# A hybrid attention and recurrence block: rotary key in two passes, cleared corners instead of a cleared tile, table loads and conditioning row rearranged

## The chip, the cores and the metric

The kernel runs on one core of a Trainium2 chip. The metric is the device time of one execution in microseconds; lower is better. The profiled execution gives a trace of every engine: TensorE (PE, with its weight loads PEld), VectorE (DVE), ScalarE (ACT), GpSimd (POOL) and SyncE (SP), which here issues nearly all DMAs.

## The reference

One layer of a block on 512 latent tokens and 256 context tokens, width 1024, all in fp32. The parts that matter here:

```python
h  = modulate(rmsnorm(x, g_norm_mix), sh1, sc1)      # mod = silu(c) @ w_mod + b_mod
cq, ckv, kpe, hq, hi, hg, ff, fb = split(h @ w_in)   # and the same for the context
# group A: latent attention, 4 heads; kpe (64 wide) is one rotary key for all heads
k_lat = full_k(kn_l, apply_rope(kpe_l, cos, sin), N) # the context's kpe is not rotated
k_ctx = full_k(kn_c, kpe_c, L)
# group B: gated linear recurrence, 4 heads, 2 directions, chunks of 64 tokens
A = einsum('bthk,bshk->bhts', qc * exp(b - b_ref), kc * exp(b_ref - b))
A = where(mask, A, 0.0)
o = rmsnorm(o_fwd + o_bwd, g_on) * silu(hg)
x = x + gt1 * (concat([o_mla, o_hgrn]) @ w_out)
x = x + gt2 * swiglu(modulate(rmsnorm(x, g_norm_ffn), sh2, sc2), w_gate, w_up, w_down)
out = rmsnorm(x, g_final)
```

`apply_rope` takes pairs of features 16 apart within 32 and rotates them by the angle of the token's row or column in the grid.

## The kernel before

**Precision by splitting.** Activations and weights stand with features on the 128 partitions. A matmul operand is split into a rounded part (hi, written by ScalarE as a cast to fp32r) and the rest (lo, written by VectorE as a difference). `mm3` (L148 to L152) multiplies hi x hi, hi x lo and lo x hi: three matmuls for one product. `make_unit` (L119) loads a weight unit of 128 x 1024 by a DMA on SyncE's queue (L122), casts it on ScalarE (L132) and takes the difference on VectorE (L133); the three tiles stand in rings of three buffers. `unit(i)` asks for two units ahead.

**Order.** The program is written in one order, and a scheduler then places each instruction in its engine's queue, by the priority of its place in the program and by when it expects it to be ready; `prio` moves a few up or down. On the chip each queue runs in order. So a line that stands far below can come early if it depends on little. PSUM gives two pairs of banks (`big`) and four single banks (`sm`).

**Stages.** (1) 0 to 65 us: modulation of the mix, the norm, h split into `hh`, `hl` (latent) and `gh`, `gl` (context). (2) 65 to 300 us: projections. `hgrn_q`, `gates` and `mla_kpe` call `project` (L452 to L465), which runs 8 k-steps; each step has three matmuls of 512 columns and three of 256. Between the steps `tick` advances generators: `hgrn_dir` (one head, one direction), `hgrn_out` (one head), `mla_feats`. (3) 300 to 360 us: scores, softmax and values of the attention, four heads. (4) the output projection, the second norm, the feed-forward layer, the last norm.

**The masked scores in `hgrn_dir`.** `pa` is a PSUM bank of four blocks of 128 x 128, each with two chunks of 64 x 64 on its diagonal. L549 multiplies a zero matrix (`zr`) by 512 columns of `hh` and so writes zero into all of the bank. Then 16 small fp32 matmuls (L555), each with 32 columns of the array and 64 or 32 columns of output, add the scores of each chunk; of each chunk one corner of 32 x 32 isn't computed, since the mask empties it. L559 copies the masked part to `am[d]`; the rest of `am` stays zero. `hgrn_out` adds the two directions on GpSimd (L592), multiplies by the values (L598 and L604), and norms (`rstd_cols`, L610 to L614); L620 turns the result round.

**`rstd_cols`** computes 1/sqrt on a few columns. With `fast` ScalarE takes a square root (L190), and VectorE takes the reciprocal and one Newton step: five VectorE instructions. Without it VectorE does all: three on the integer bits, then three Newton steps of three: twelve. Here `fast` is on in the last head only.

**The rotary key, `mla_kpe` (L709 to L720).** The last unit of `w_in` (KPU) has 128 columns: the 64 of kpe, and the same 64 with features exchanged 16 apart. One `project` gives both. VectorE multiplies the first half by cos (L713) and the second by sin (L714), ScalarE moves the second to the partitions of the first (L715), VectorE adds them (L716). Then the result is split into `krh` (L719) and `krl` (L720), for latent and context apart and into both halves of the partitions.

**The conditioning row.** `scx` holds silu(c) on all partitions, 128 x 1024, in the place of the cos and sin tables. L433 loads c as a broadcast, L434 and L435 make silu of it; `late_mod` (L422 to L429) then multiplies rows of `w_mod` by it, one row of 128 x 1024 each. After 12 of these the tables are loaded over it (L746). When the queries are rotated (L786 to L794) c is loaded again and silu made again (L812 to L815), for the other 20.

**Function tables of ScalarE.** Sigmoid, Exp, Sqrt and Silu need different tables; a table load precedes the first use after another. Two lines are there to load a table early: L818 (Exp, before the softmax) and L1037 (Sqrt, before the last norm).

## Time and profile before

| | |
|---|---|
| median of 3 runs (lowest to highest) | 793.59 us (791.45 to 795.61) |
| profiled execution: its time | 792.62 us |
| its span (first to last instruction) | 790.8 us |
| mean granted clock of TensorE | 0.988 |
| instructions: TensorE, VectorE, ScalarE | 4342, 820, 569 |
| DMA traffic | 88.77 MB |

The page of a profile gives busy times by engine, a picture of the span in 40 slices, the chain of work that ended last (followed back from the end, at each step to what released it), and groups of instructions by line. Further views give the same for a stretch of time: busy time of each engine, who waited for whom, and single instructions in order. A matmul's recorded length overlaps with its neighbours; the distance from one start to the next is what a matmul costs in a full stream.

### The profile page before, as it was taken

What the parts mean: (1) busy time and instruction counts of PE and PEld (TensorE: products, weight loads), DVE (VectorE), ACT (ScalarE), POOL (GpSimd) and SP (SyncE); (2) the same over time, 40 slices, a digit from 0 to 9 for tenths busy, and PEclk for the clock granted to TensorE, in tenths of its full rate; (3) what the DMA queues carried; (4) which work ended last, traced back from release to release, by engine and by line L of the source; (5) the groups of instructions that cost most, each with busy time, mean ns of one, the idle gap of its engine ahead of it and who ended that gap; (6) DMA issues with size and microseconds to landing.
All of it is one profiled execution on the core that took longest, in us unless ns stands there. A gap on an engine that the chain in (4) does not pass through costs nothing.

```text
span 790.8 us, 10832 instructions
## 1 busy us (share of the span) xinstructions
PE 768.1 (97%) x4342; PEld 631.7 (80%) x4342; DVE 446.9 (57%) x820; ACT 311.4 (39%) x569; POOL 10.1 (1%) x18
## 2 busy tenths in 40 slices
PE   8899999999999989999999999999999999999995
PEld 7568878788887768888999888888888888888885
DVE  5576569839778989985566434432333233223324
ACT  6344246434544577664344223222322222212211
POOL 0000000000000100000000000000000000000000
PEclk8899999999999999999999999999999999999997
DMA  9923723311110022345403343423232323332303
GB/s 332 390 76 134 252 80 108 133 57 55 64 55 28 28 80 90 125 165 181 160 2 100 113 160 133 151 89 107 80 107 82 104 78 96 93 100 80 111 3 107
DMA packets 26706, 88.77 MB, mean 112 GB/s; under 512 B 2976, under 2 KB 5280, under 8 KB 26528
## 3 DMA queue, kind: packets, MB, share of 16 engines
q1 hardware_dynamic: 25568, 87.03, 33.0%
q10 hardware_dynamic: 1088, 1.05, 0.4%
q8 instruction: 34, 0.56, 0.3%
q14 instruction: 16, 0.13, 0.1%
HBM read 85.97 MB, written 2.10 MB: 111 GB/s over the span
## 4 chain that ended last, share of the span: by engine, by line
PE 89%; DVE 7%; ACT 2%; issue 1%; DMA 1%; SPq 0%; DVEq 0%; ACTq 0%
PE big L150 18%; PE big L151 17%; PE big L152 17%; PE sm L150 9%; PE sm L151 9%; PE sm L152 9%; PE big L857 2%; PE sm L604 1%; PE sm L876 1%; PE big L858 1%; PE sm L320 1%; DVE U L585 1%; PE sm L598 1%; DVE acl L309 1%; DVE G L506 1%
## 5 line engine op out<-in xcount | busy, mean ns | idle before, releaser
L133 DVE TENSOR_TENSOR wl<-wf,wh 128x1024 fp32r<-128x1024 f32 (+2 forms) x100 | 119.6, 1196 | 186.3 <-ACT wh L132 186.2
L132 ACT CAST wh<-wf 128x1024 fp32r<-128x1024 f32 (+2 forms) x100 | 102.9, 1029 | 280.3 <-PE big L151 167.6
L150 PE MATMUL big<-h2h,wh 128*128 128x512 f32 (+1 forms) x368 | 140.3, 381 | 0.0
L151 PE MATMUL big<-h2l,wh 128*128 128x512 f32 (+1 forms) x368 | 140.0, 381 | 0.0
L152 PE MATMUL big<-h2h,wl 128*128 128x512 f32 (+1 forms) x368 | 140.0, 381 | 0.0
L151 PEld LDWEIGHTS big<-h2l,wh 128*128 128x128 f32 x368 | 69.2, 188 | 14.6
L150 PEld LDWEIGHTS big<-h2h,wh 128*128 128x128 f32 x368 | 69.2, 188 | 14.4
L152 PEld LDWEIGHTS big<-h2h,wl 128*128 128x128 f32 x368 | 69.2, 188 | 14.4
L150 PE MATMUL sm<-ah,wh 128*128 128x512 f32 (+1 forms) x198 | 73.5, 371 | 0.0
L152 PE MATMUL sm<-ah,wl 128*128 128x512 f32 (+1 forms) x198 | 73.4, 371 | 0.0
L151 PE MATMUL sm<-al,wh 128*128 128x512 f32 (+1 forms) x198 | 73.4, 370 | 0.0
L427 DVE SCALAR_TENSOR_TENSOR wl<-wl,cs 128x1024 f32<-128x1024 f32 x32 | 39.0, 1220 | 33.8 <-DMA wl<-in_wmt_dram 33.8
L150 PE MATMUL big<-wh,hh 128*128 128x512 f32 x96 | 40.2, 422 | 3.3 <-ACT hh L340 1.9
L150 PEld LDWEIGHTS sm<-ah,wh 128*128 128x128 f32 x198 | 37.3, 188 | 7.1
L151 PEld LDWEIGHTS sm<-al,wh 128*128 128x128 f32 x198 | 37.3, 188 | 7.1
L152 PEld LDWEIGHTS sm<-ah,wl 128*128 128x128 f32 x198 | 37.3, 188 | 7.1
L150 PE MATMUL big<-hh,wh 128*128 128x512 f32 x104 | 42.8, 412 | 0.0
L151 PE MATMUL big<-hl,wh 128*128 128x512 f32 x104 | 40.9, 394 | 0.0
L152 PE MATMUL big<-hh,wl 128*128 128x512 f32 x104 | 40.8, 392 | 0.0
L151 PE MATMUL big<-wl,hh 128*128 128x512 f32 x96 | 38.8, 406 | 0.0
L152 PE MATMUL big<-wh,hl 128*128 128x512 f32 x96 | 38.4, 402 | 0.0
L506 DVE RECIPROCAL G<-S 128x528 f32<-128x528 f32 x8 | 27.5, 3432 | 0.1
(326 smaller groups left out, 1353.4 us busy)
## 6 DMA issues: line engine op xcount, KB each, us to landing
wf<-in_wgu_dram SPq DMA_DIRECT2D x44, 512.0 KB, 3.4
wl<-in_wmt_dram SPq DMA_DIRECT2D x32, 512.0 KB, 3.5
wf<-in_wi_dram SPq DMA_DIRECT2D x25, 512.0 KB, 3.9
wf<-in_wd_dram SPq DMA_DIRECT2D x16, 512.0 KB, 3.5
wms<-in_wm_dram SPq DMA_DIRECT2D x11, 512.0 KB, 9.6
wf<-in_wo_dram SPq DMA_DIRECT2D x8, 512.0 KB, 3.5
wf<-in_wd_dram SPq DMA_DIRECT2D x8, 384.0 KB, 3.1
wm<-in_wm_dram SPq DMA_DIRECT2D x5, 512.0 KB, 10.2
```

The costliest lines, as they stand in the source:

```text
L132: nc.scalar.copy(hi[:, :w], f[:, :w])
L133: nc.vector.tensor_sub(lo[:, :w], f[:, :w], hi[:, :w].bitcast(F32))
L150: nc.tensor.matmul(o, lh, rh, start=start, stop=False, skip_group_check=True)
L151: nc.tensor.matmul(o, lh, rl, start=False, stop=False, skip_group_check=True)
L152: nc.tensor.matmul(o, ll, rh, start=False, stop=stop, skip_group_check=True)
L309: nc.vector.tensor_add(acc_, acc_, sq_)
L320: nc.tensor.matmul(ps[32 * g : 32 * g + 32, :256], csil[:, 4 * j + kk, :], f[:, kk * 256 : (kk + 1) * 256], start=(j == 0), stop=(j == 1), ...
L427: nc.vector.scalar_tensor_tensor(f, f, 1.0, sc, op0=ALU.mult, op1=ALU.mult, accum_out=acc)
L506: nc.vector.reciprocal(I, S)
L585: nc.vector.scalar_tensor_tensor(U[:, c1, :], U[:, c0, :], er[:, 1, c0 : c0 + 1], U[:, c1, :], op0=ALU.mult, op1=ALU.add)
L598: nc.tensor.matmul(t, a2[:, j, :], vt[:, j, h * P : (h + 1) * P], start=True, stop=False, skip_group_check=True)
L857: nc.tensor.matmul(ps[:, 0, :], L, R[:, :NL], start=(i == 0), stop=(i == 4), skip_group_check=True)
```

## The change

- **Rotary key.** The KPU unit holds only the 64 columns of kpe, and its hi and lo parts stand side by side in one tile of 128 columns per k-step. Two matmuls instead of three (by `hh` and by `hl`, or `gh` and `gl`) give the hi products on the lower 64 partitions and the lo products on the upper 64; the sum of both halves is the key, now with lo x lo as well. The exchange of features 16 apart is a shuffle on VectorE behind it, and latent and context are split together, 768 columns at a time. An Exp with scale 0 into a spare column follows the rotation.
- **Corners.** Instead of L549 two bf16 matmuls with zeros write the corner blocks alone, and the small matmuls overwrite instead of adding. The masked copy is made for the two diagonal quarters apart.
- **Norm of the last head.** `fast` is off.
- **Conditioning row.** After the first silu one row of it goes to a scratch row in DRAM; the second load reads that row as a broadcast, and the second Sigmoid and product go, with the Exp behind them (L818).
- **L1037** goes.

```diff
@@ units, make_unit
-        units.append(("wi", wi[u], UNIT))
+        units.append(("wi", wi[u], UNIT) if u < NW_IN - 1 else ("kp", wi[u][:, : UNIT // 2], UNIT // 2))
...
-        nc.scalar.copy(hi[:, :w], f[:, :w])
-        nc.vector.tensor_sub(lo[:, :w], f[:, :w], hi[:, :w].bitcast(F32))
+        if kind == "kp":
+            f3 = f[:, :w].rearrange("p (k c) -> p k c", c=64)
+            h3 = hi.rearrange("p (k s c) -> p k s c", s=2, c=64)
+            nc.scalar.copy(h3[:, :, 0], f3)
+            nc.vector.tensor_sub(h3[:, :, 1], f3, h3[:, :, 0].bitcast(F32))
+        else:
+            nc.scalar.copy(hi[:, :w], f[:, :w])
+            nc.vector.tensor_sub(lo[:, :w], f[:, :w], hi[:, :w].bitcast(F32))
@@ conditioning row, first time
+    srow = tc.dram_tile([1, DM], F32, name="srow")
...
     nc.vector.tensor_mul(scx, scx, scs)
+    nc.sync.dma_start(srow, scx[0:1, :])
...
-    zr = HG.tile([P, P], F32R, name="zr")
-    nc.gpsimd.memset(zr.bitcast(F32), 0.0)
+    zr = HG.tile([P, P], F32, name="zr")
+    nc.gpsimd.memset(zr, 0.0)
     zc = zr.bitcast(BF16)
@@ hgrn_dir
         pa = sm()
-        nc.tensor.matmul(pa, zr, hh[:, 0, :], start=True, stop=False, skip_group_check=True)
+        for g in (1 - d, 3 - d):
+            c0 = (g // 2) * CH + 32 * d
+            nc.tensor.matmul(pa[32 * g : 32 * g + 32].rearrange("p (j t) -> p j t", t=P)[:, :, c0 : c0 + 32],
+                             zc[:, 0:32], zc[:, 0:P].rearrange("p (j t) -> p j t", t=32), start=True, stop=True,
+                             skip_group_check=True, tile_position=(0, 32 * g))
...
-                                 start=False, stop=True, skip_group_check=True, tile_position=(0, 32 * g))
+                                 start=True, stop=True, skip_group_check=True, tile_position=(0, 32 * g))
         with prio(100):
             p4 = pa.rearrange("p (j t) -> p j t", t=P)
-            nc.vector.copy_predicated(am[d], mk[:, d : d + 1, :].to_broadcast([P, 4, P]), p4)
+            for g in range(2):
+                r = slice(g * CH, (g + 1) * CH)
+                nc.vector.copy_predicated(am[d][r, :, r], mk[r, d : d + 1, r].to_broadcast([CH, 4, CH]), p4[r, :, r])
@@ hgrn_out
-        rr, _ = rstd_cols(HG, (ss, 4), P, fast=h == NH - 1)
+        rr, _ = rstd_cols(HG, (ss, 4), P)
@@ mla_kpe
-        ps = project(KPU)
-        kp = HG.tile([P, NL], F32, tag="q", name=nm("kp"), bufs=2)
-        m = HG.tile([P, NL], F32, tag="sg", name=nm("kpm"), bufs=2)
-        nc.vector.tensor_mul(kp[0:64, :], ps[0:64, :NL], C("cos")[0:64, :])
-        nc.vector.tensor_mul(kp[64:128, :], ps[64:128, :NL], C("sin")[64:128, :])
-        nc.scalar.copy(m[0:64, :], kp[64:128, :])
-        nc.vector.tensor_add(kp[0:64, :], kp[0:64, :], m[0:64, :])
-        for src, c in ((ps[0:64, NL:NT], slice(NL, NT)), (kp[0:64, :], slice(0, NL))):
-            for r in (slice(0, 64), slice(64, 128)):
-                nc.scalar.copy(krh[r, c], src)
-                nc.vector.tensor_sub(krl[r, c], src, krh[0:64, c].bitcast(F32))
+        w, _ = unit(KPU)
+        ps = big()
+        for k in range(KT):
+            for i in range(2):
+                for o, n, t in ((ps[:, 0, :], NL, (hh, hl)), (ps[:, 1, :NC], NC, (gh, gl))):
+                    nc.tensor.matmul(o, w[:, k * P : (k + 1) * P], t[i][:, k, :n], start=(k == 0 and i == 0),
+                                     stop=(k == KT - 1 and i == 1), skip_group_check=True)
+            if k in (1, 4):
+                tick()
+        ps = ps.rearrange("p a b -> p (a b)")
+        kp = HG.tile([P, NT], F32, tag="kk", name=nm("kp"), bufs=3)
+        m = HG.tile([P, NT], F32, tag="sg", name=nm("kpm"), bufs=2)
+        nc.scalar.copy(m[0:64, :], ps[64:128, :NT])
+        nc.vector.tensor_add(kp[0:64, :], ps[0:64, :NT], m[0:64, :])
+        nc.vector.stream_shuffle(m[0:64, :NL], kp[0:64, :NL], SWAP)
+        nc.vector.tensor_mul(kp[0:64, :NL], kp[0:64, :NL], C("cos")[0:64, :])
+        nc.vector.tensor_mul(m[0:64, :NL], m[0:64, :NL], C("sin")[0:64, :])
+        nc.vector.tensor_add(kp[0:64, :NL], kp[0:64, :NL], m[0:64, :NL])
+        nc.scalar.activation(epst2[0:64, :], m[0:64, 0:1], AF.Exp, scale=0.0)
+        for r in (slice(0, 64), slice(64, 128)):
+            nc.scalar.copy(krh[r, :], kp[0:64, :])
+            nc.vector.tensor_sub(krl[r, :], kp[0:64, :], krh[0:64, :].bitcast(F32))
@@ behind make_qr
-    nc.sync.dma_start(scx, cin.rearrange("(o c) -> o c", o=1).to_broadcast([P, DM]))
-    scs = HG.tile([P, DM], F32, tag="U", name="scs", bufs=2)
-    nc.scalar.activation(scs, scx, AF.Sigmoid)
-    nc.vector.tensor_mul(scx, scx, scs)
+    nc.sync.dma_start(scx, srow.to_broadcast([P, DM]))
     lim_[0] = 32
     wq_n = unit(QU + 2, 1)
-    nc.scalar.activation(epst2, scs[:, 0:1], AF.Exp)
@@ before the last norm
-    nc.scalar.activation(epst2, epst, AF.Sqrt)
@@ host: the last unit of w_in
-    wi += [_tiles(np.concatenate([kp, kp[:, swap]], axis=1))[0]]
+    wi += [np.zeros((P, UNIT), np.float32)]
+    wi[-1][:, : UNIT // 2] = kt(part["kpe"]).reshape(P, UNIT // 2)
```

3 lines of the change are left out of this document (removed).

## The prediction

> **What bounds the kernel now.** I read the page first: busy time, then the chain of work that ended last.
>
> ```profile
> PE 768.1 (97%) x4342; PEld 631.7 (80%) x4342; DVE 446.9 (57%) x820; ACT 311.4 (39%) x569; POOL 10.1 (1%) x18
> ...
> PE 89%; DVE 7%; ACT 2%; issue 1%; DMA 1%; SPq 0%; DVEq 0%; ACTq 0%
> ```
>
> TensorE is busy 97% of the span and makes up 89% of the chain, so matmul time taken out should come off the end, except where another engine sets the pace. The places that the change touches lie between 100 and 303 us, so I read busy time by stretch there (columns after the stretch and its length: busy us of TensorE, its weight loads, VectorE, ScalarE, GpSimd, each with its count of instructions; then the granted clock, the DMA share, and GB/s).
>
> ```profile
> 100.00:231.00 131.00, 129.71 (x897) 107.52 (x897) 100.74 (x196) 59.21 (x132) 2.57 (x2) 1.00 0.25 79
> ...
> 251.40:271.00 19.60, 17.96 (x177) 14.58 (x173) 18.99 (x43) 10.20 (x31) 1.27 (x1) 1.00 0.02 5
> 271.00:285.00 14.00, 13.98 (x77) 10.02 (x79) 12.93 (x26) 7.83 (x16) 2.30 (x3) 1.00 0.21 68
> 285.00:293.50 8.50, 6.36 (x29) 4.17 (x26) 7.56 (x17) 7.91 (x18) 0.00 (x0) 1.00 0.42 136
> ```
>
> Up to 231 us TensorE is full (129.71 of 131 us) and VectorE has room (100.74). From 251.4 to 285 VectorE is as full as TensorE (31.92 and 31.94 of 33.6 us). From 285 to 293.5 all three engines leave gaps: waits in a row, not one full engine. The granted clock is 1.00 throughout. Who TensorE waits for from 225 to 310 us (waiter, releaser: total us, times, longest):
>
> ```profile
> PE big L150 <- DVE krl L720: 1.6, 1, 1.6
> PE sm L620 <- DVE ow L614: 1.2, 1, 1.2
> PE big L857 <- ACT pp L863: 1.1, 1, 1.1
> PE big L150 <- DVE qnl L776: 1.0, 2, 0.7
> ```
>
> All four name VectorE or ScalarE. The chain of waits agrees: between these two pieces (start, us, what) it stays on VectorE, for 19.5 us, and goes on on TensorE.
>
> ```profile
> 251.44 0.70 DVE qg L531
> ...
> 270.49 0.43 DVE krl L720
> ```
>
> **The change part by part.**
>
> *Clearing the corners of the masked scores (L549).* This runs eight times. Today a 512-column multiplication by zeros comes before the 16 small ones; the chain shows it as follows (start, us, what).
>
> ```profile
> 130.15 0.24 PE sm L549
> 130.39 0.58 PE sm L555 x22
> 130.97 0.43 PE big L150
> ```
>
> L549 puts 0.24 us on the chain. It goes; two bf16 clears of 128 columns come, each on a quarter of the array's columns. No row shows such an instruction. From above: the two cost as much as L549 and the gain is nothing; a loss I exclude, since together they send half of its columns. From below: L555's 16 multiplications take 0.58 us, two of that kind 0.07; and L150 behind L555 takes 0.43 where L549, as wide, takes 0.24, so a change of kind costs some 0.19, which may go too. I take 0.11 for the two, nearest to L555, whose tile positions they share: 0.13 us saved each time. Five of the eight lie where TensorE sets the end (130 to 228 us): 5 x 0.13 = **0.65 us**, bounds 0 to 5 x (0.24 - 0.07 + 0.19) = 1.8. The copy behind it (L559, 0.71 us in the table of VectorE below) becomes two of 64 x 256; by the 256-wide L720 (0.412) that is 0.82, or 0.11 more VectorE time each.
>
> *Rotary key in two passes.* One of eight k-steps of the projection today, its first matmul and that of the next step:
>
> ```profile
> 255.99 0.39 PE L150 MATMUL big<-hh,wh 128*128 128x512 f32 x1
> ...
> 257.03 0.40 PE L150 MATMUL big<-hh,wh 128*128 128x512 f32 x1
> ```
>
> Six matmuls take 1.04 us; four take two thirds, 0.69. Over eight steps 0.35 x 8 = 2.8 us of TensorE go. But they lie at 251 to 264 us, where VectorE is the chain. So VectorE's bill decides. Its rows (mean ns of one is the last number before the next bar):
>
> ```profile
> L559 DVE COPY_PREDICATED am<-mk,sm 128x512 f32<-128x512 int32 x8 | 5.7, 710 | 0.0
> ...
> L861 DVE TENSOR_REDUCE ast<-big 128x1 f32<-128x768 f32 x4 | 3.8, 950 | 0.9 <-PE big L858 0.9
> ...
> L182 DVE SCALAR_TENSOR_TENSOR rsr<-rst,rsr 128x4 f32<-128x4 f32 x16 | 2.6, 161 | 0.3
> ...
> L716 DVE TENSOR_TENSOR kp<-kp,kpm 64x512 f32<-64x512 f32 x1 | 1.4, 1416 | 0.0
> ...
> L720 DVE TENSOR_TENSOR krl<-kp,krh 64x512 fp32r<-64x512 f32 x2 | 1.4, 685 | 0.0
> ...
> L788 DVE SCALAR_TENSOR_TENSOR m<-m,cs 128x512 f32<-128x512 f32 x2 | 1.4, 682 | 0.0
> ...
> L815 DVE TENSOR_TENSOR cs<-cs,scs 128x1024 f32<-128x1024 f32 x1 | 1.2, 1212 | 0.0
> ...
> L720 DVE TENSOR_TENSOR krl<-big,krh 64x256 fp32r<-64x256 f32 x2 | 0.8, 412 | 0.0
> ```
>
> Out: L713 and L714 (512 wide, as L788: 0.68 each), L716 1.416, L720 twice 0.412 and twice 0.685: 5.0 us. In: the sum of the halves over 768 columns (as L861, 0.95), a shuffle, two products and a sum of 512 (as L788, 0.68 each), two differences of 768 (0.95 each): 5.6 us. That is +0.6. ScalarE's copies grow from 2048 to 2304 columns in all, and a table load joins them; ScalarE is busy 10.20 of 19.60 us there, which hides both. What queues behind that load are the copies of the key and of the values (L802); if the cover were gone, it would cost the load's 1.28 us and some 0.3 for the columns. The KPU unit's split is half as wide: it falls near 222 us, where both engines have room, so I count nothing. A gain no instruction shows: today the PSUM pair of the projection is held until the last L720 that reads it, and TensorE waits 1.6 us for that; after, the first sum frees it.
>
> L716's 1.416 us is twice a 512-wide sum (L788 0.682), and this stands beside it:
>
> ```profile
> 267.18 1.27 POOL L592 TENSOR_TENSOR a<-am,am 128x512 f32<-128x512 f32 x1 [27.58 <-DVE am L559]
> ```
>
> The sum of head 3 ran on GpSimd from 267.18 to 268.45, and L716 from 267.58: they met. [...]
>
> *Last head's norm without the square root.* `rstd_cols` in head 3 goes from one ScalarE and five VectorE steps to twelve VectorE steps of 0.16 us (L182): seven more, 1.12 us if nothing lies between, about half of that when they alternate with long instructions. I count +0.5. The step is on the path: L614 at 293.02 needs it, and TensorE waits 1.2 us at L620 for L614.
>
> *Conditioning row and table loads.* ScalarE's rows:
>
> ```profile
> 287.49 1.28 ACT L190 ACT_TABLE_LOAD   x1
> ...
> 297.88 1.28 ACT L1037 ACT_TABLE_LOAD   x1
> ...
> 300.60 1.28 ACT L863 ACT_TABLE_LOAD   x1 [1.22 <-DVE ast L861]
> 301.89 0.90 ACT L863 ACTIVATE pp<-big,ast 128x768 f32<-128x768 f32 x1
> ```
>
> Five table loads of 1.28 us lie from 287.5 to 301.9 us. L190 delays the second query copy, hence the wait on qnl. The exponential prepared at L818 is thrown away by L1037: the scheduler has put that square root, written far below, at 297.88, and so L863 loads again, between the first reduce and the first softmax. TensorE waits 1.1 us for this (gap 1.25 us to its next start). After, one load stands in the key path and none of these five. L863 starts 1.28 us earlier: **1.25 us**, bounds 0 (another table comes between) to 1.28. With L1037 nothing is lost for the norm at the end, which it was written for: L863's load at 300.60 undoes it already.
>
> [...]
>
> L815 (1.21 us of VectorE) and its Sigmoid go; the row is read from the scratch row in the same 512 KB broadcast. The store adds one small DMA on SyncE's queue, which must wait for L435:
>
> ```profile
> 68.80 1.22 DVE L435 TENSOR_TENSOR cs<-cs,scs 128x1024 f32<-128x1024 f32 x1
> ```
>
> ```profile
> 71.18 7.48 SPq L425 DMA_DIRECT2D wl<-in_wmt_dram  x5
> ```
>
> L435 ends at 70.02, and the next load on that queue leaves at 71.18, so the store fits in between; behind it are only loads of later rows. I count nothing; bound: L435's 1.2 us, on a load that nobody waits for at once.
>
> *The stretch from 251.4 to the first score reduce, taken together.* VectorE's waits there:
>
> ```profile
> DVE vl L803 <- ACT vh L802: 0.6, 1, 0.6
> ...
> DVE ast L861 <- PE big L858: 0.4, 1, 0.4
> DVE wl L133 <- ACT wh L132: 0.4, 1, 0.4
> DVE qnl L776 <- ACT qnh L775: 0.3, 1, 0.3
> DVE onl L623 <- ACT onh L622: 0.3, 1, 0.3
> ```
>
> L803 and L133 wait for late matmuls, L776 and L623 for ScalarE's tables, L861 for the scores: 2.0 us that can go. The bill: +0.6 (key) + 3 x 0.11 (corners) + 0.5 (norm) - 1.21 (L815) = +0.2; with one meeting with GpSimd more (1.416 - 0.682 = 0.73) +0.9. I use +0.6, between them: 2.0 - 0.6 = 1.4 us. More is possible, since L133 at 297.89 (1.23 us) prepares an output weight that the first scores don't need: 2.6.
>
> ```profile
> 293.02 1.12 DVE L614 SCALAR_TENSOR_TENSOR ow<-sm,rsr,shg 128x128 f32<-128x128 f32 x4
> ...
> 297.89 1.23 DVE L133 TENSOR_TENSOR wl<-wf,wh 128x1024 fp32r<-128x1024 f32 x1
> 299.56 0.96 DVE L861 TENSOR_REDUCE ast<-big 128x1 f32<-128x768 f32 x1 [0.44 <-PE big L858]
> ```
>
> I take the middle, **2.0 us**. Bounds: 0.3, where the bill is +0.9 and 1.2 of the waits go, and rival 1. So the 2.8 us of matmuls don't come off as such; what comes off is the waits that they cause on VectorE.
>
> Sum: 0.65 + 2.0 + 1.25 = 3.9 us. The profiled execution took 792.62 us (span 790.8 and 1.8 around it), which becomes 788.7. The median of the runs is 793.59, 0.97 higher; against that I forecast **789.7 us**.
>
> **Rivals.**
> 1. *TensorE bounds the stretch after all.* Its 97% speaks for it, and so does that VectorE's low-priority work there could move later. Then all removed matmuls count, 2.8 + 8 x 0.13 = 3.8, with the waits on krl (1.6), qnl (1.0) and pp (1.1): 7.5 us, 786.1.
> 2. *VectorE swallows the stretch.* Its 18.99 of 19.60 us speaks for it: gain there 0.3 instead of 2.0: 0.65 + 0.3 + 1.25 = 2.2, 791.4.
> 3. *The prepared exponential doesn't last*: another hoisted table function comes in between, as L1037 did. The change then doesn't do what it says: 0.65 + 2.0 = 2.65, 790.9. Against it: no square root is left that depends on nothing.
> 4. *Slower: VectorE's queue ahead of the first score reduce.* The conditioning row is ready sooner without L815 and its Sigmoid, so the scheduler may put late modulation rows (as wide as L815, 1.21 us, three staging buffers: 3.6) ahead of the reduce, and the norm's twelve steps between long instructions (12 x 0.68 = 8.2 us instead of the 5.5 from L190 to L614 now: 2.7). With the key (0.6), the corners (0.3) and a second meeting with GpSimd (0.73), less L815: 6.7 us of work in place of the gain of 2.0, less 1.9 elsewhere: 4.8 slower, 798.4. The kernel is slower from 1.9 us of such work on, and by over 0.5% from 5.9. Against it: these rows were behind the scores before.
>
> **How the numbers follow.** A measurement of this kernel tells about 0.5% (4.0 us) from no change, so the forecast stands on the border. Chances: forecast 0.46 (own range 788.4 to 791.0, 0.22 of it over the border), rival 1 0.25, rival 2 0.14, rival 3 0.07, rival 4 0.08. Faster by over 0.5%: 0.22 + 0.25 = 0.47; within: 0.24 + 0.14 + 0.07 = 0.45; slower: 0.08. The range reaches rivals 1 to 3 with the bounds of the clears (about 1 us either way): 785.5 to 792.5.
>
> **What would show it.** Right: no table load between 280 and 303 us; 32 matmuls for the key instead of 48; the wait on krl gone; VectorE over 95% busy from the key to the scores; that stretch 2 us shorter. Wrong: TensorE without gaps there (rival 1), or twelve norm steps ending after 293 us (rival 4).

## The result and the profile after

The changed kernel takes 800.22 us (median of 5 runs, 798.88 to 800.70); the kernel before took 793.00 us beside it (5 runs, 791.45 to 795.61). The ratio is 1.0088, 95% interval 1.0070 to 1.0107: slower by some 7 us. The profiled execution took 800.31 us, with a span of 798.5 us and a mean granted clock of 0.982 (before: 790.8 us and 0.988). Lines move: what was L150 to L152 is L156 to L158, L585 is L599, L559 is L573, L614 is L628, L620 is L634, L776 is L799, L133 is L139, L861 is L880, L863 is L882.

The page of the changed kernel, busy time and chain by engine:

```profile
PE 765.9 (96%) x4334; PEld 629.2 (79%) x4334; DVE 449.4 (56%) x835; ACT 305.6 (38%) x560; POOL 10.8 (1%) x18
...
PE 84%; DVE 8%; DMA 4%; ACT 2%; issue 1%; SPq 0%; DVEq 0%; ACTq 0%
```

TensorE is busy 2.2 us less than before, and the span is 7.7 us longer: the time is lost in gaps. Who TensorE waits for from 225 to 310 us (waiter, releaser: total us, times, longest):

```profile
PE sm L634 <- DVE ow L628: 7.2, 1, 7.2
PE big L156 <- DVE vl L826: 1.4, 1, 1.4
PE sm L547 <- DVE rst L186: 1.2, 1, 1.2
PE sm L618 <- DVE U L599: 1.0, 1, 1.0
PE big L156 <- DVE kp L735: 0.9, 1, 0.9
```

The waits on krl and pp are gone, as predicted; waits on vl, on rst and on kp (the sum that now frees the PSUM pair) have come in their place. And the wait of the last head's transposes for `ow`, 1.2 us before, is now 7.2 us. Busy time by stretch (columns as in the prediction), first the kernel before, then the changed one:

```profile
285.00:295.00 10.00, 7.85 (x38) 5.41 (x35) 9.06 (x20) 9.39 (x19) 0.00 (x0) 1.00 0.36 116
295.00:305.00 10.00, 8.90 (x52) 7.61 (x51) 8.17 (x14) 8.73 (x16) 0.00 (x0) 1.00 0.17 63
```

```profile
285.00:295.00 10.00, 7.51 (x51) 5.09 (x50) 9.35 (x19) 7.19 (x17) 0.00 (x0) 1.00 0.28 95
295.00:305.00 10.00, 5.29 (x18) 4.54 (x19) 7.59 (x21) 1.60 (x4) 0.00 (x0) 0.50 0.45 136
```

From 295 to 305 us the granted clock is 0.50 where it was 1.00, and half of that time TensorE works. Its instructions around the wait (start, us, engine, line, operation, and in brackets the idle time before):

```profile
292.11 0.40 PE L158 MATMUL big<-cq,wl 128*128 128x512 f32 x1
299.71 0.66 PE L634 MATMUL sm<-cs,ow 128*128 128x128 f32 x2 [7.20 <-DVE ow L628]
...
301.87 0.63 PE L156 MATMUL sm<-ck,wh 128*128 128x512 f32 x1
302.30 0.63 PE L157 MATMUL sm<-ck,wh 128*128 128x512 f32 x1
302.72 0.63 PE L158 MATMUL sm<-ck,wl 128*128 128x512 f32 x1
```

Behind the wait 512-column matmuls start 0.43 us apart; in the full stream before they stood 0.23 apart. Now VectorE in that time, the last head's norm from its second step on:

```profile
293.13 0.16 DVE L203 TENSOR_SCALAR rsi<-rsv 128x4 int32<-128x4 int32 x1
293.20 1.22 DVE L139 TENSOR_TENSOR wl<-wf,wh 128x1024 fp32r<-128x1024 f32 x1
294.34 0.16 DVE L204 TENSOR_SCALAR rsr<-rsi 128x4 int32<-128x4 int32 x1
294.41 0.69 DVE L799 SCALAR_TENSOR_TENSOR qnl<-big,qnh 128x512 fp32r<-128x512 f32 x1
295.01 0.15 DVE L186 TENSOR_TENSOR rst<-rsr 128x4 f32<-128x4 f32 x1
295.19 0.69 DVE L817 TENSOR_TENSOR qs<-m,qs 64x512 fp32r<-64x512 f32 x1
295.91 0.16 DVE L187 SCALAR_TENSOR_TENSOR rst<-rst,rsv 128x4 f32<-128x4 f32 x1
296.10 0.69 DVE L817 TENSOR_TENSOR qs<-m,qs 64x512 fp32r<-64x512 f32 x1
296.82 0.16 DVE L188 SCALAR_TENSOR_TENSOR rsr<-rst,rsr 128x4 f32<-128x4 f32 x1
296.90 1.22 DVE L139 TENSOR_TENSOR wl<-wf,wh 128x1024 fp32r<-128x1024 f32 x1
...
299.21 1.12 DVE L628 SCALAR_TENSOR_TENSOR ow<-sm,rsr,shg 128x128 f32<-128x128 f32 x4
```

Each small step depends on the one in front of it, and into each gap up to 298 us the scheduler has put the next long instruction that is ready; the last six steps follow one another 0.2 us apart. The fourth qnl and the second L139 here stood behind ow in the kernel before (295.19 and 297.89 us). TensorE stays idle for all of them.

**Where the time goes.** The start of the program differs from one execution to the next, so I measure from the first copy of vt. These rows are the marks of the changed kernel (those of qg, ow and the first score reduce of the kernel before, 251.44, 293.02 and 299.56, stand in the prediction), and the row of before that the prediction doesn't show follows:

```profile
69.23 0.69 DVE L413 COPY vt<-big 128x512 f32<-128x512 f32 x1 [2.06 <-PE big L158]
...
252.96 0.69 DVE L539 TENSOR_TENSOR qg<-qt,S 128x512 f32<-128x512 f32 x1 [2.74 <-PE sm L618]
...
307.51 0.95 DVE L880 TENSOR_REDUCE ast<-big 128x1 f32<-128x768 f32 x1
```

```profile
68.19 0.69 DVE L407 COPY vt<-big 128x512 f32<-128x512 f32 x1 [2.06 <-PE big L152]
```

The same marks in every run's profile, in us (the wait is TensorE's at the last transposes). The median and the ratio are of all executions of a run. Each ratio is an estimate against the executions of the kernel before in the same round, whose median was 793.1 us (e1 to e4), 791.9 (e5 to e8), 794.0 (e9 to e12) and 793.3 (e13 to e16); it isn't the quotient of the two medians.

| kernel | vt to last ow | ow to first reduce | vt to first reduce | reduce to end | wait | median, us | ratio to before (95%) |
|---|---|---|---|---|---|---|---|
| before | 224.8 | 6.5 | 231.4 | 491.2 | 1.2 | 793.0 | |
| after | 230.0 | 8.3 | 238.3 | 491.0 | 7.2 | 800.2 | 1.0088 (1.0070 to 1.0107) |
| e1 | 228.8 | 8.1 | 236.9 | 492.0 | 6.1 | 801.8 | 1.0096 (1.0063 to 1.0128) |
| e2 | 230.9 | 7.9 | 238.9 | 491.2 | 7.2 | 799.2 | 1.0071 (1.0047 to 1.0096) |
| e3 | 228.5 | 8.3 | 236.8 | 491.5 | 5.8 | 800.3 | 1.0084 (1.0051 to 1.0116) |
| e4 | 225.6 | 9.9 | 235.5 | 491.0 | 4.7 | 798.6 | 1.0071 (1.0045 to 1.0098) |
| e5 | 229.6 | 6.0 | 235.7 | 491.0 | 1.4 | 796.7 | 1.0051 (1.0022 to 1.0079) |
| e6 | 231.0 | 7.9 | 238.9 | 490.9 | 3.2 | 801.7 | 1.0115 (1.0082 to 1.0148) |
| e7 | 225.8 | 10.9 | 236.7 | 491.3 | none | 799.0 | 1.0079 (1.0050 to 1.0109) |
| e8 | 224.8 | 6.8 | 231.6 | 491.5 | 1.2 | 795.5 | 1.0029 (1.0005 to 1.0052) |
| e9 | 226.7 | 8.9 | 235.6 | 492.1 | 3.0 | 799.9 | 1.0074 (1.0046 to 1.0101) |
| e10 | 229.7 | 8.3 | 238.0 | 491.2 | 6.1 | 800.6 | 1.0097 (1.0070 to 1.0125) |
| e11 | 225.1 | 8.9 | 234.1 | 491.4 | 2.6 | 796.0 | 1.0033 (1.0010 to 1.0055) |
| e12 | 224.8 | 7.2 | 232.0 | 490.9 | none | 794.4 | 1.0009 (0.9990 to 1.0028) |
| e13 | 224.8 | 6.5 | 231.3 | 491.4 | 1.2 | 793.1 | 1.0002 (0.9982 to 1.0021) |
| e14 | 230.1 | 8.2 | 238.3 | 491.6 | 7.2 | 799.8 | 1.0089 (1.0059 to 1.0118) |
| e15 | 230.4 | 6.0 | 236.4 | 491.7 | 1.3 | 797.1 | 1.0052 (1.0033 to 1.0071) |
| e16 | 226.1 | 7.5 | 233.5 | 491.7 | none | 793.3 | 1.0009 (0.9987 to 1.0030) |

The marks are those of one profiled execution each. That of e8 is the fastest of its ten (789.32 us; the others took 792.64 to 797.28) and that of e16 the slowest of its twelve (797.37), so these two speak less for their run.

Behind the first reduce almost nothing changes (491.2 and 491.0). The loss is 6.9 us between vt and the first reduce: 5.2 in front of ow, 1.8 behind it.

**VectorE's bill in front of ow.** From the seventh masked-score copy to the last ow I sum the starts-to-starts of all VectorE instructions:

| us, and count | before | after | e3 norm alone | e4 key alone | e9 one pad | e10 three pads |
|---|---|---|---|---|---|---|
| length | 36.1 | 40.7 | 39.7 | 36.9 | 37.9 | 41.0 |
| idle in it | 2.2 | 2.5 | 2.3 | 2.6 | 2.2 | 2.3 |
| key (kp, kpm, krl) | 4.85 | 6.47 | 4.84 | 5.38 | 4.84 | 4.84 |
| masked copies (am) | 1.21 | 1.80 | 1.19 | 1.20 | 1.20 | 1.18 |
| norm steps, two heads | 1.75 | 2.69 | 2.42 | 1.86 | 1.80 | 1.81 |
| weight splits (wl) | 3.57 x3 | 4.56 x4 | 4.69 x4 | 4.72 x4 | 3.57 x3 | 4.70 x4 |
| qnl | 1.80 x3 | 2.47 x4 | 2.42 x4 | 2.48 x4 | 1.79 x3 | 2.39 x4 |
| L815 | none | none | 1.13 | none | 1.11 | 1.13 |

VectorE is nearly full in all six, with 2.2 to 2.6 us of idle time (the sums are good to some 0.2 us). Of the 4.6 us that after has more, 3.2 are the change's own work (key 1.6, norm 0.9, copies 0.6) and 1.7 are the fourth split and the fourth qnl, which were behind ow and have moved in front of it; the U steps take some 0.3 less.

Most of the delay is there before the last norm begins: its first step stands 223.2 us behind vt instead of 218.8, and from it to ow it takes 6.8 us instead of 6.0. In e3, with the old key, the norm begins at 218.8 and takes 9.6 us: there the long instructions stand inside it.

### The profile page after: what moved, and what is told of

Its sections match the earlier page's. It is cut to its first block, busy times and chain, and to the rows that moved or that the text cites. A ratio compares the mean times of both kernels' runs of the same rounds, so it can differ in the third digit from the quotient of the medians.

```text
span 798.5 us, 10830 instructions
## 1 busy us (share of the span) xinstructions
PE 765.9 (96%) x4334; PEld 629.2 (79%) x4334; DVE 449.4 (56%) x835; ACT 305.6 (38%) x560; POOL 10.8 (1%) x18
## 4 chain that ended last, share of the span: by engine, by line
PE 84%; DVE 8%; DMA 4%; ACT 2%; issue 1%; SPq 0%; DVEq 0%; ACTq 0%
PE big L156 16%; PE big L157 16%; PE big L158 15%; PE sm L156 9%; PE sm L157 9%; PE sm L158 9%; DMA wms<-in_wm_dram 2%; PE big L876 2%; PE sm L618 1%; DVE wl L139 1%; PE sm L895 1%; PE big L877 1%; DMA wm<-in_wm_dram 1%; DVE G L514 1%; DVE U L599 1%
## 5 line engine op out<-in xcount | busy, mean ns | idle before, releaser
L139 DVE TENSOR_TENSOR wl<-wf,wh 128x1024 fp32r<-128x1024 f32 (+1 forms) x99 | 118.4, 1196 | 186.6 <-ACT wh L138 186.6
L138 ACT CAST wh<-wf 128x1024 fp32r<-128x1024 f32 (+1 forms) x99 | 101.8, 1028 | 276.1 <-PE big L157 164.5
L156 PE MATMUL big<-h2h,wh 128*128 128x512 f32 (+1 forms) x368 | 140.3, 381 | 0.0
L158 PE MATMUL big<-h2h,wl 128*128 128x512 f32 (+1 forms) x368 | 140.0, 381 | 0.0
L156 PEld LDWEIGHTS big<-h2h,wh 128*128 128x128 f32 x368 | 69.2, 188 | 14.6
L158 PEld LDWEIGHTS big<-h2h,wl 128*128 128x128 f32 x368 | 69.2, 188 | 14.5
L156 PE MATMUL sm<-ah,wh 128*128 128x512 f32 (+1 forms) x198 | 73.5, 371 | 0.0
L158 PE MATMUL sm<-ah,wl 128*128 128x512 f32 (+1 forms) x198 | 73.4, 371 | 0.0
L156 PE MATMUL big<-wh,hh 128*128 128x512 f32 x96 | 40.2, 422 | 4.2 <-ACT hh L346 1.9
L156 PEld LDWEIGHTS sm<-ah,wh 128*128 128x128 f32 x198 | 37.3, 188 | 7.1
L158 PEld LDWEIGHTS sm<-ah,wl 128*128 128x128 f32 x198 | 37.3, 188 | 7.1
L156 PE MATMUL big<-hh,wh 128*128 128x512 f32 x96 | 39.6, 412 | 0.0
L158 PE MATMUL big<-wh,hl 128*128 128x512 f32 x96 | 38.5, 402 | 0.0
L157 PE MATMUL big<-hl,wh 128*128 128x512 f32 x96 | 37.8, 394 | 0.0
L158 PE MATMUL big<-hh,wl 128*128 128x512 f32 x96 | 37.7, 392 | 0.0
L156 PEld LDWEIGHTS big<-wh,hh 128*128 128x128 f32 x96 | 18.2, 192 | 12.3 <-ACT hh L346 3.6
```

The source lines that it names most:

```text
L138: nc.scalar.copy(hi[:, :w], f[:, :w])
L139: nc.vector.tensor_sub(lo[:, :w], f[:, :w], hi[:, :w].bitcast(F32))
L156: nc.tensor.matmul(o, lh, rh, start=start, stop=False, skip_group_check=True)
L157: nc.tensor.matmul(o, lh, rl, start=False, stop=False, skip_group_check=True)
L158: nc.tensor.matmul(o, ll, rh, start=False, stop=stop, skip_group_check=True)
```

## Experiments

The first four runs were made under a first theory, that the last head's longer norm makes the loss by itself; the letters in their expectations belong to that round. From the fifth on, A is the theory that stood up in the end: VectorE's queue in front of ow, and the clock behind the wait.

**e1: the square root back in the changed kernel.**

```diff
-        rr, _ = rstd_cols(HG, (ss, 4), P)
+        rr, _ = rstd_cols(HG, (ss, 4), P, fast=h == NH - 1)
```

> The changed kernel with the square root back in the last head's norm; all else as changed. Theory A (the norm's twelve VectorE steps, queued between long instructions, hold TensorE at the transposes of the last head for 7.2 us, and its clock falls behind that): 789 to 793 us, TensorE's wait at the transposes at most 2 us, granted clock from 285 to 303 us back at 1.00; one or two table loads more, 1 to 2.5 us of the gain. Theory B (the new key path delays the last head, and the norm only stands where this shows): 796 us or more, the wait moves to another line.

Ratio 1.0096 (1.0063 to 1.0128): nothing comes back. That refutes the first theory's 789 to 793 us: the norm alone isn't the cause. ow comes 1.2 us earlier, the wait is still 6.1 us.

**e2: the norm's steps with a higher priority.**

```diff
-        rr, _ = rstd_cols(HG, (ss, 4), P)
+        with prio(400 if h == NH - 1 else 0):
+            rr, _ = rstd_cols(HG, (ss, 4), P)
```

> The changed kernel, with the last head's norm given a higher priority, so that its twelve VectorE steps stand together in the queue and no weight split lies between them; no arithmetic changed. Theory A: the steps take about 2.4 us instead of 6.6, TensorE's wait at the transposes falls from 7.2 to 3 us or less, 789 to 794 us. Theory B: 796 us or more.

VectorE's queue came out the same, instruction by instruction, so this is a second run of the changed kernel: 1.0071 (1.0047 to 1.0096). A priority doesn't close the gaps between dependent steps; it only decides who is first among what is ready.

**e3 and e4: one part alone, from the kernel before** (e3: `fast` off in the last head; e4: the two-pass key with its unit and its shuffle).

> The kernel before with nothing changed but the last head's norm without the square root. Theory A: 3 to 8 us slower than before, with a long wait of TensorE at the transposes. Theory B: within 1.5 us of before, since the key path is the old one.

> The kernel before with the two-pass key alone (weights side by side, sum, shuffle, rotation; no early exponential). Theory A: 3 us faster to 1 us slower than before. Theory B: 4 to 7 us slower, the last head's products with U and qg start 3 us or more later than before.

Each alone costs about as much as all together: 1.0084 (1.0051 to 1.0116) and 1.0071 (1.0045 to 1.0098). The costs don't add. e3 also refutes theory B (within 1.5 us of before), as e1 did A. With the norm alone, L815, the fourth split and the fourth qnl move in front of ow (2.9 us). With the key alone ow is only 0.8 us later, but TensorE, with the key's matmuls saved, comes to this wait 2.7 us earlier (221.4 us behind vt instead of 224.1). It waits 4.7 us, its clock is 0.50 from 295.4 to 302.2 us, and ow to first reduce grows from 6.5 to 9.9.

**e5: TensorE kept busy in the wait of the changed kernel.**

```diff
         make_q(h)
         tick()
+    pf = big()[:, 0, :]
+    with prio(400):
+        for i in range(18):
+            nc.tensor.matmul(pf, qnh[:, 2, 0:P], qnh[:, 3, :], start=True, stop=True, skip_group_check=True)
     drain()
```

> The changed kernel with 18 extra 512-column matmuls on TensorE (their product is thrown away) between the last query projection and the last head's transposes, in the 7.2 us in which TensorE waits for the norm. Nothing is added on VectorE. Theory A (VectorE's work ahead of the last ow sets when the transposes start, +4.7 us against before; the idle TensorE then runs at half the granted clock for some 5.3 us, +2.3 us): ow stays where it is, the granted clock stays above 0.95 from 285 to 310 us, ow to first score reduce falls from 8.3 to about 6 us, and the time falls by about 2 us, to 797 to 799 us, still slower than before by some 4 to 5 us. Rival B (the low clock is a mere companion of the wait, or comes from elsewhere): no gain, 800 us or more, since 4.1 us of matmuls are added.

As A has it: 1.0051 (1.0022 to 1.0079). The stretches of e5:

```profile
285.00:295.00 10.00, 8.60 (x56) 6.07 (x55) 9.34 (x20) 6.46 (x17) 0.00 (x0) 1.00 0.24 81
295.00:305.00 10.00, 8.64 (x46) 6.97 (x45) 7.61 (x21) 1.65 (x3) 0.00 (x0) 1.00 0.33 104
```

ow stays where it was (229.6 against 230.0), the clock stays at 1.00, and ow to first reduce falls from 8.3 to 6.0. 18 useless matmuls make the kernel faster (796.7 us, where it took 800.2).

**e6 and e7: the last U first**, in e7 with the square root of e1 as well.

```diff
-        with prio(-100):
+        with prio(100 if (h, d) == (NH - 1, 1) else -100):
             U = HG.tile([P, NCH, P], F32, tag="U", name=nm("U"), bufs=2)
```

> The changed kernel with the last head's second U chain no longer put off in the scheduler's order (priority +100 instead of -100 for that one block). The U steps then stand 5.4 us of VectorE work earlier in the queue, but the work in front of the last ow falls only from 35.7 to 34.4 us by the durations of the trace, because the norm's twelve steps still alternate with long instructions (15.3 us between U and ow instead of 11.2). Theory A: ow comes 1 to 1.5 us earlier, the wait of TensorE stays over 4 us, the clock still halves: 798.5 to 800 us. Rival D (the last U being late is the cause by itself): ow comes some 5 us earlier, 793 to 795 us.

> As the kernel with U first, and the last head's norm again with the square root on ScalarE (six steps in place of twelve on VectorE, two more table loads on ScalarE). VectorE's work in front of the last ow is 28.8 us, 6.9 less than in the changed kernel and 2.1 less than before; 4.7 us of it comes behind ow and in front of the first reduce instead. Theory A: TensorE's wait at the transposes falls under 3 us, the clock stays above 0.95, and the time comes to 791 to 795 us. Rival D (U alone decides): the same as the run with U first, within 1 us. Rival E (the whole of VectorE's work up to the first reduce decides, 38.4 us here against 36.4 before and 40.6 after, wherever it stands): 796 to 797 us.

e6 refutes D: U ends some 5 us earlier, but ow comes later (231.0), since the norm's steps now alternate with long instructions to the end (10.6 us from the first step to ow). A's 798.5 to 800 was missed as well (801.7): I had summed VectorE's durations, and left out its waits, which grow from 2.5 to some 5 us in front of ow (1.9 us for vh and 1.5 for the norm's input are the longest). In e7 ow is nearly where it was before (225.8), and TensorE doesn't wait there. Yet it takes 799.0, not 791 to 795. What had been pushed behind ow now stands in front of the first scores:

```profile
299.88 0.69 DVE L799 SCALAR_TENSOR_TENSOR qnl<-big,qnh 128x512 fp32r<-128x512 f32 x1
300.60 1.40 DVE L817 TENSOR_TENSOR qs<-m,qs 64x512 fp32r<-64x512 f32 x2
302.03 1.23 DVE L139 TENSOR_TENSOR wl<-wf,wh 128x1024 fp32r<-128x1024 f32 x1
303.18 1.94 DVE L792 TENSOR_TENSOR knl<-sm,knh 128x512 fp32r<-128x512 f32 x4
305.85 0.96 DVE L880 TENSOR_REDUCE ast<-big 128x1 f32<-128x768 f32 x1 [0.73 <-PE big L877]
```

The scores need knl, and knl stands last. So ow is not the only door; the whole of VectorE's work up to the scores (rival E) bounds the stretch as soon as ow doesn't. E's 796 to 797 us was still too low.

**e8: the conditioning row alone**, from the kernel before (the scratch row, the Exp in the key path, L1037 gone).

> The kernel before with one part of the change: the conditioning row kept in a scratch row (no second Sigmoid, no L815), the exponential's table loaded in the key path, the square root of L1037 gone; single clears, the three-pass key and the norm with the square root stay. L815 (1.21 us of VectorE) stood behind the last ow in the kernel before. Theory A: work behind ow isn't on the path, so nothing of the 1.21 us comes off; since the norm's square root still replaces the exponential's table, the load in front of the first softmax stays: 792 to 793.5 us, same. The prediction's own bill (every VectorE instruction of that stretch counts alike): 1.2 us faster, 791.8; with the exponential prepared as well 2.5 us faster, 790.5.

1.0029 (1.0005 to 1.0052): nothing gained. ow (224.8) and the first reduce (231.6 against 231.4) stay; L815 stood behind ow, beside TensorE's own work, and without it VectorE waits 2.3 us for the first scores instead of 0.4. Why the ratio is a little above 1, where theory A had no change, the marks don't show: the profiled execution had a mean granted clock of 0.994, the other nine 0.984 to 0.990.

**e9 and e10: added VectorE work in the kernel before**, one and three instructions whose result ow overwrites.

```diff
         w = HG.tile([P, 4, P], F32, tag="rs_d", name=nm("ow"), bufs=1)
+        gh = shg[:, :, h * P : (h + 1) * P]
+        if h == NH - 1:
+            for _ in range(1):
+                nc.vector.scalar_tensor_tensor(w, gh, rr[:, 0:1], gh, op0=ALU.mult, op1=ALU.mult)
```

> The kernel before, with one more 512-wide VectorE instruction (0.6 us) between the last head's norm and ow; what it writes is overwritten by ow, so the output is the reference's. In VectorE's queue L815 (1.2 us) slips in between it and ow, having stood behind ow. Theory A (VectorE's work in front of the last ow, and half a clock for some 5.3 us once TensorE has idled over 3 to 4 us): ow 1.8 us later, TensorE's wait 1.2 + 1.8 = 3.0 us, the clock from 285 to 310 us stays 1.00: 1.8 us slower, 794 to 796 us. A rival by which only an instruction's own time counts: 0.6 us slower, not to be told from no change.

> As the run with one added instruction, with three (1.8 us). Each depends on nothing but takes its turn in front of ow, and L815, a qnl (0.6 us) and a weight split L133 (1.15 us) slip in between. Theory A: ow 4.8 us later, TensorE's wait 6.0 us, the clock halves for some 5 us after it (2.6 us more): 7 us slower, 799 to 801 us, four times the cost of one for three times the work. The rival by which only their own time counts: 1.8 us slower, 795 us.

One instruction of 0.75 us makes the kernel 1.0074 (1.0046 to 1.0101) slower. The mechanism shows in e9's queue:

```profile
295.48 0.75 DVE L616 SCALAR_TENSOR_TENSOR ow<-shg,rsr 128x512 f32<-128x512 f32 x1
296.14 1.22 DVE L819 TENSOR_TENSOR cs<-cs,scs 128x1024 f32<-128x1024 f32 x1
297.28 1.12 DVE L618 SCALAR_TENSOR_TENSOR ow<-sm,rsr,shg 128x128 f32<-128x128 f32 x4
```

L819 (L815 of before) slipped in, and ow came 1.9 us later, as expected. The size was missed: the theory's 3 to 4 us was an estimate between the 1.4 us of e5, where the clock held, and the 4.7 us of e4, where it fell, and a wait of 3.0 us was already enough to halve the clock.

```profile
295.00:299.00 4.00, 1.23 (x8) 1.04 (x9) 3.96 (x8) 3.96 (x6) 0.00 (x0) 0.99 0.03 10
299.00:302.00 3.00, 3.00 (x12) 2.62 (x12) 2.13 (x3) 2.73 (x5) 0.00 (x0) 0.50 0.24 49
302.00:303.00 1.00, 1.00 (x5) 0.85 (x4) 0.78 (x2) 0.17 (x1) 0.00 (x0) 0.85 0.92 373
```

It falls when TensorE is already back at work (from 297.8). Besides, TensorE waits 2.8 us for the first softmax instead of 1.1, which fits the 0.9 us more behind the first reduce. e10 did as expected (1.0097, 1.0070 to 1.0125): 2.0 us of added work pull three long instructions in front of ow. But it isn't four times as dear as one, since one already pays for a halved clock (3.4 us of it in e9, 6.8 in e10).

**e11: the corners alone**, from the kernel before (both parts of it, clears and copies).

> The kernel before with the corners alone: two bf16 clears in place of the wide one, and the two copies of 64 by 256 in place of one of 128 by 512. VectorE's work in front of the last ow is 0.6 us more, with the same instructions behind ow as before. Theory A: 0.6 us slower there, against at most 0.65 us saved on TensorE up to 228 us: 792 to 794 us, the same. The prediction's term: 0.65 us faster.

1.0033 (1.0010 to 1.0055), 2 us slower where I expected none. The clears do save TensorE time: from the last small matmul in front of them to the first projection matmul behind the scores it is 0.79 us instead of 1.02, so 0.23 saved each time. But at ow nothing has come of it (225.1 against 224.8), since TensorE waits for VectorE more instead: 0.7 us for shg, which the kernel before didn't wait for, and 1.0 us instead of 0.6 for U.

```profile
PE sm L610 <- DVE U L591: 1.0, 1, 1.0
PE big L150 <- DVE shg L644: 0.7, 1, 0.7
```

That is 1.1 us of waits against 5 x 0.23 us saved. And TensorE's wait for ow is 2.6 us, and the clock is 0.50 from 295 to 298 us:

```profile
292.00:294.00 2.00, 0.00 (x0) 0.00 (x0) 1.87 (x6) 1.97 (x3) 0.00 (x0) 1.00 0.04 16
294.00:295.00 1.00, 0.67 (x4) 0.55 (x4) 1.00 (x5) 1.00 (x2) 0.00 (x0) 0.80 0.00 0
295.00:298.00 3.00, 3.00 (x11) 2.34 (x11) 2.25 (x3) 2.64 (x5) 0.00 (x0) 0.50 0.00 0
```

**e12 and e16: versions meant to be faster**, from the kernel before: the scratch row, and the first head's key matmuls in front of the last transposes.

```diff
     for h in range(NH):
         make_q(h)
         tick()
+    kb = big()
+    k0 = [k_mm(0, 0, NL, kb[:, 0, :]), k_mm(0, NL, NC, kb[:, 1, :NC])]
     drain()
```

e12 loads the exponential's table behind the last head's square root, e16 behind the first head's key copies; e16 has the filled start of e13 too.

> A version for speed, from the kernel before: the conditioning row in a scratch row (L815 and its Sigmoid gone), the norm with the square root kept, the exponential's table loaded right behind that square root, and the first head's key matmuls (12, 2.1 us) put in front of the last head's transposes, into the wait. Single clears and the three-pass key stay. VectorE's work in front of ow is as before (30.9 us). Theory A: 1.25 us for the table and 1.2 to 2 us for the matmuls: 789.5 to 791 us, 2.5 to 3.5 us faster than before. Rival E (all of VectorE's work up to the first reduce decides): 1.2 us faster from L815 alone plus the table, 790.5; the matmuls bring nothing.

> A version for speed, from the kernel before: the start filled as above, the conditioning row in a scratch row, the first head's key matmuls in front of the last head's transposes, and the exponential's table loaded behind the first head's key copies, where ScalarE waits for the first reduce (in the run before it the load stood ahead of onh and held it up). Norm with the square root, three-pass key and single clears as before. Theory A: ow to first reduce 5 to 6 us instead of 6.5, so 0.5 to 1.5 us under the kernel before with the start filled: 788 to 790, the fastest so far. What the earlier table load brings behind the first reduce is expected to be absorbed, since in the changed kernel the fourth reduce came 0.8 us earlier and the twelfth at the same distance.

Neither beats the kernel before (1.0009, 0.9990 to 1.0028, and 1.0009, 0.9987 to 1.0030), and both expectations were missed. The wait is gone, but ow to first reduce is 7.2 and 7.5 us instead of 6.5: the scores now wait for ScalarE's key copies (knh, 0.7 us in both). The key's matmuls weren't the bound there.

**e13 to e15: the start.** Executions of one kernel spread over up to 8 us, and the first vt copy stood between 64.4 and 71.8 us, so a part of the 7 us might have been an accident of the start. 22 more matmuls on ones fill it, in before (e13), after (e14) and e5 (e15).

```diff
+    warm(10)
     dg = rstd_diag(A, cols)
     abs_ = [modsel(0, sb)]
+    warm(6)
     pb = rstd_spread(dg)
+    warm(6)
```

> The kernel before with 22 more warm-up matmuls on ones among the first statistics (10 to 28 us), so that TensorE has fewer gaps there; nothing else changes. In the profiles so far the first vt copy stands anywhere from 64.4 to 71.8 us, late where the granted clock of 10 to 30 us is low. Theory A (the clock halves after a nearly idle stretch of some 3 us, wherever it is): the clock of 10 to 30 us stays over 0.95, the first vt copy comes at 64 to 66.5 us, the runs of this kernel spread over less than 4 us, and the median falls by 2 to 4 us, to 789 to 791. If the spread has another cause: no change, 792 to 794.

> The changed kernel with the same 22 matmuls. If the start is drawn alike in both kernels and the change's loss lies wholly between the last copies of head 3's masked scores and the first score reduce, the distance to the kernel before with these matmuls stays 6 to 7.5 us: 796 to 798. If a part of the 7 us was drawn at the start: a smaller distance, 3 to 5 us.

> The changed kernel with the same 22 matmuls at the start and the 18 throw-away matmuls in the wait for the last ow. Theory A: 2.3 to 2.8 us under the changed kernel with the start filled alone, the clock from 285 to 310 us 1.00, and still 4 to 4.7 us over the kernel before with the start filled, which is VectorE's work in front of ow.

The expectation of e13 was missed: the median doesn't fall (1.0002, 0.9982 to 1.0021), and vt comes at 68.45 us. But 10 of its 12 runs lie between 792.8 and 793.4, where the 29 runs of the kernel before lie between 788.5 and 796.3. With this the distance of the two kernels is 799.75 - 793.13 = 6.6 us: it is the change's, not the start's. e15 takes the halved clock behind the wait out: 799.75 - 797.07 = 2.7 us. The remaining 797.07 - 793.13 = 3.9 us go with the later ow (230.4 us behind vt against 224.8), which is VectorE's queue.

## Why the prediction was wrong

**The term that failed** is "The stretch from 251.4 to the first score reduce, taken together": -2.0 us by the prediction, +6.4 measured (from qg to the first reduce 48.1 us before, 54.6 after; the other 0.5 of the 6.9 lies ahead of qg). Three things in it were wrong.

- **The end of the stretch.** The prediction summed VectorE's work up to the first reduce as one bill. But as long as TensorE waits for ow, only what stands in front of ow counts. L815, credited with 1.21 us, stood at 294.06, behind ow at 293.02, in a row that could be read: in e8, without it, the first reduce comes no earlier. Without that credit the bill is +1.4 us by the prediction's own numbers, not +0.2.
- **The order was taken as given.** The norm was costed at +0.5 us for seven steps of 0.16. A dependent step can cost what is put in front of the next one. "More is possible, since L133 at 297.89 prepares an output weight that the first scores don't need": such an instruction moved forward instead, with the fourth qnl, 1.7 us in all. e3, e9 and e10 show it apart from the rest.
- **"2.0 us of waits that can go."** VectorE's idle time in front of ow is 2.2 us before and 2.5 after. Where waits went, others came: in the changed kernel 1.1 us for the last masked scores (L567), which the kernel before doesn't have.

**What was missing** is the clock. The prediction read 1.00 throughout and took it as given; a longer wait was costed at its own length. It costs the halved clock behind it as well: 2.3 us from ow to the first reduce (8.3 in after, 6.0 in e5), 2.7 us of time (e14 against e15). The clock fell to 0.50 behind the gap of 7.2 us, and behind gaps of 3.0 (e9) and 2.6 us (e11) at the same place; behind a gap of 2.8 us 13 us later in e9, in the wait for the first pp, it stayed at 1.00. So no fixed length decides it here.

Even 1.4 us can be enough. e2 runs the same instructions as the changed kernel, and both wait 1.4 us for vl; the clock halves behind this wait in e2 and not in the changed kernel. In each of the 18 traces the changes of the granted clock stand whole multiples of 3.41 us apart (in the changed kernel it is 1.00 for 269.65 us, 79 of them, up to 294.90, and then 0.50 for 10.24 us, 3 of them), so I lay stretches of that length on this grid, first for the changed kernel, then for e2:

```profile
271.00:274.42 3.42, 2.63 (x14) 1.62 (x12) 3.39 (x5) 2.40 (x4) 0.37 (x1) 1.00 0.01 2
274.42:277.83 3.41, 2.72 (x11) 1.91 (x11) 3.36 (x6) 3.13 (x8) 0.85 (x1) 1.00 0.43 154
```

```profile
268.48:271.89 3.41, 1.97 (x12) 1.11 (x11) 3.38 (x6) 3.21 (x5) 0.00 (x0) 1.00 0.01 2
271.89:275.30 3.41, 3.41 (x9) 2.64 (x9) 2.67 (x5) 2.22 (x7) 1.63 (x2) 0.50 0.48 154
```

In the changed kernel the wait (273.7 to 275.1) is split between two stretches; in e2 (270.3 to 271.7) one stretch has all of it, and the clock falls at its end. In the stretch before a fall TensorE was busy for 0.81 us in e11, 1.02 in the changed kernel and 1.12 in e9; no stretch with less than 1.5 us kept the clock at 1.00. Between 1.6 and 2.5 us it fell in some traces (1.77 in e16, 1.97 in e2, 2.45 in the kernel before at its start, at 13.9 us) and held in others (1.66 in e10, 1.96 in e9, 1.99 in the kernel before at its wait of 1.2 us). So in these traces the fall goes less with the length of a wait than with how much work it leaves in one stretch of this grid, and where the grid falls differs from one execution to the next (a stretch begins at 271.00 us in the changed kernel, at 268.48 in e2).

**The meeting with GpSimd** came. The sum of head 3 ran beside one product of the new key, and both took longer (GpSimd's 1.27 us before):

```profile
269.67 1.69 POOL L606 TENSOR_TENSOR a<-am,am 128x512 f32<-128x512 f32 x1 [28.54 <-DVE am L573]
```

```profile
270.14 1.77 DVE L738 TENSOR_TENSOR kpm<-kpm,cs 64x512 f32<-64x512 f32 x1
...
272.61 0.67 DVE L739 TENSOR_TENSOR kp<-kp,kpm 64x512 f32<-64x512 f32 x1
```

One instruction pays 1.1 us, and that is most of the key's +1.6; in e4, where they hardly meet (the sum runs from 268.90 to 270.17, this product from 270.64, and it takes 0.67), the key costs +0.5, as the prediction's +0.6 had it. No run shows the second meeting that the prediction's +0.9 and rival 4 count at 0.73 us; the changed kernel has this one.

**Corners, -0.65 us:** each time 0.23 us of TensorE were saved where 0.13 was counted, but none of it comes off the end (e11). The step that failed is that "TensorE sets the end" from 130 to 228 us: VectorE's shg and U took up what was saved. The copies cost a little more than counted: two take 0.90 us together, where the prediction had 0.82 and one took 0.71.

**Exponential, -1.25 us:** no table load stands between 280 and 303 us any more, and the softmax starts without one.

```profile
271.99 1.28 ACT L740 ACT_TABLE_LOAD   x1 [1.09 <-DVE kpm L738]
...
308.56 0.90 ACT L882 ACTIVATE pp<-big,ast 128x768 f32<-128x768 f32 x1 [3.51 <-DVE ast L880]
```

The fourth score reduce comes 7.5 us after the first instead of 8.3. But the twelfth stands 40.3 us behind it in both kernels. The step was right and its gain absorbed: 0.2 us are left (491.2 to 491.0). What takes the place of "TensorE waits 1.1 us for this" further on isn't shown.

**The rivals.** Rival 4 (slower, 798.4, a chance of 0.08) had the place and the sign, and its pieces came: the norm between long instructions, the key, the corners, a meeting with GpSimd. Two late modulation rows came too, ahead of the first reduce (at 301.52 and 306.36 us), but behind ow, where VectorE waited anyway. That the total of 798.4 lies near the measured 800.2 is in part luck: it counted 3.6 us for these rows, which cost some 0.2 (the reduce starts 0.25 us behind the end of its last matmul instead of 0.04), took L815 off, and lacked the clock. The argument against it, "these rows were behind the scores before", spoke against one piece only and didn't hold for that one, and "twelve norm steps ending after 293 us" was the right sign to name. Rival 1 (TensorE bounds all) had the largest chance of the others, and is refuted by the 7.2 us in which TensorE does nothing. Rival 2 named the right engine but allowed it no loss.

**What stays open.** The times of e6, e7 and e8 lie about 2 us over what the marks of their one profile give; why is not known. A halved clock that their profile doesn't show could make such a difference; that isn't shown. Which measure of TensorE's work the clock goes by is open too: recorded busy time draws no sharp border. A version of the changed kernel without the meeting on GpSimd was not tried. No version that was run beats the kernel before.

## What to carry to other kernels

Where an engine waits for the end of a chain of small dependent steps in another engine's queue, count what stands in the queue in front of the chain's last step, and expect a list scheduler to put one ready long instruction in front of each dependent step: an added step can cost that instruction (0.69 to 1.22 us here), not its own 0.16 us. Work behind the step that releases the wait is worth nothing when removed (e8, 1.0029), as long as nothing behind that step bounds in its turn (e7). And when TensorE is freed, look where it will then stand idle: the stall of 7.2 us here was paid again as a halved clock, 2.7 us (e14 to e15), and the norm and the key alone, with stalls of 5.8 and 4.7 us, each cost about as much as all together (1.0084 and 1.0071 against 1.0088).

## What the runs showed of the hardware

- The granted clock went from 1.00 to 0.50 at waits of TensorE for ow of 2.6 us (e11), 3.0 (e9), 4.7 (e4), 5.8 (e3), 6.1 (e1, e10) and 7.2 (the changed kernel), and at one of 1.4 us for vl in e2; not at 1.2 for ow (the kernel before), at the 2.8 us for pp in e9, or at the same 1.4 us for vl in the changed kernel. Its changes stand whole multiples of 3.41 us apart in each trace (10.24 and 269.65 us in the changed kernel), and the work that TensorE has in such a stretch goes with the fall better than the length of the wait (0.81, 1.02 and 1.12 us in front of the falls in e11, the changed kernel and e9; 1.99 at the wait of the kernel before, where it held). In e9 and e11 it stayed there for about 3.4 us, in the changed kernel for about 10 (294.9 to 305.1), and in e9 it fell about 1 us after the work had begun again.
- At the clock of 0.50 a 512-column matmul costs 0.43 us instead of 0.23 (the changed kernel, behind and in front of its wait for ow). 18 matmuls whose product is thrown away, put into the wait, took 2.7 us off (e14 to e15).
- Much of the spread between executions of the kernel before comes from the start: filling it drew 10 of 12 into 0.6 us (e13), where the 29 without it lie between 788.5 and 796.3.
- A VectorE product of 64 x 512 took 1.77 us beside a GpSimd sum of 128 x 512 (the changed kernel, L738), and 0.67 without (the same product in e4).
